# A fourth column chunk of gate and up by seven products, and one written-out order for all units

## The chip, the cores and the metric

The kernel runs on one core of one Trainium2 chip. The metric is device microseconds of one execution, as the median of several. The engines are named as in the profile: PE is the matrix engine (TensorE; PEld is its loading of the stationary operand), DVE is VectorE, ACT is ScalarE, POOL is GpSimd, and SP is SyncE, which here only issues transfers.

## The reference, cut to what matters

One decoder layer on 256 tokens of width 1024: attention and a convolution side by side, an output projection, and a gated feed-forward part. The change touches the last line alone.

```python
D_MODEL = 1024
SEQ = 256
D_FF = -(-8 * D_MODEL // (3 * 256)) * 256        # 2816

    x = x + jnp.concatenate([attn, conv], axis=-1) @ w_out[l]
    h = rms_norm(x, norm2_g[l])
    x = x + (jax.nn.silu(h @ w_gate[l]) * (h @ w_up[l])) @ w_down[l]
```

## The kernel before

**Arithmetic.** Everything is float32 in and out. PE multiplies in a reduced float32 form, so each operand is split into a rounded high part and the rest, and one product of a 128-row block is three matmuls: high by high, high by low, low by high (`product`, L729 to L735). The activations stand still in PE, the weights move through in 512 columns. The activations are 256 tokens, so two token blocks (i = 0, 1); the width of 1024 is two halves (kh = 0, 1) of four blocks of 128.

**Weights.** They come from HBM as blocks of 128x2048 (1 MB), issued by SP into a ring of four buffers (`raw`) or, for three of the four blocks of a shared chunk, into one of three home buffers (`big_h`, `big_l`, `side`). Each block has two pieces of 128x1024. `feed` (L271) prepares pieces ahead of PE: ACT copies the piece to its rounded high part (`wh`, L278), DVE subtracts that from the piece to get the rest (`wl`, L283). Both go into rings of seven buffers (`WGT`), and `feed(at + LEAD)` asks ahead of a unit for the piece four places on. When the second piece of a block is through, the next load is issued.

**Units.** The feed-forward part is a row of units, each 12 matmuls of 128x512. The 2816 columns of gate and up are cut into chunks of 512, 512, 512, 256, 512 and 512 (`WIDTHS`, numbered 0 to 5):

- A plain chunk of 512 is 8 units `("g", c, z, kh, a)`: gate or up (z), half of the width (kh), one piece each. They add into banks `fg`. Chunk 3, of 256 columns, has gate and up in one block: 4 units `("h", 3, 0, kh, a)`.
- A shared chunk takes gate and up of both token blocks by seven products instead of eight (Winograd's form of Strassen's): units `("s", c, j)`, j = 0 to 6, two pieces each. The banks are U (products 0, 2, 4, 6), V (1, 5) and W (3). The four weight blocks are b11, b21 (gate) and b12, b22 (up). Product 0 uses b11, product 3 b21, product 5 b22. Products 1 and 2 use b11 + b12 and that sum plus b22, made by DVE in place (L277). Product 4 uses b12 + b22, and product 6 the sum of all four with b21: these two are made by accumulating transfers that POOL issues (L291), two pieces each. Between products ACT copies U and V out (`s`, L867), and DVE combines them (`c`, L872, L878, L885).
- The down projection is 22 rows `("f", f)` of 128 columns of the activations, one piece each, adding into four banks `pd`. The last four rows wait until the end and are then done bank by bank.

Once gate and up of a chunk are there, ACT takes the silu (`sf`, `sg`, L807), DVE multiplies (`ac`, L822), PE turns the result by transposes (`aT`, L813), ACT copies it (`act`, L816) and DVE makes its low part (`act`, L818); the rows f of that chunk need them.

**Order.** Python's order of these calls is the order on every engine: nothing is moved afterwards. `_order` (L71) writes the units; `_plan` derives from it the list of pieces, which loads follow which piece, and which home a block takes. A home passes from a chunk to the next: after product 4 its buffer takes the next chunk's b11, after product 5 the next b12, after product 6 the next b22. `_order` writes all of chunk 0 plain, then three stages, each with a shared chunk woven into others by a string of turns:

```python
    stage(1, chunk(2), "spspspspspspspp")
    stage(4, half + rows(0, 8), MIXED)
    stage(5, rows(8, 16), "spspspspspspspp")
    return order + rows(16, NF)
```

The banks of U and V, of `aT` and W, and of `fg` and `pd` come from pools of two, two and four; a bank can be written anew only when its last reader is through. Small delays such as `EVICT` count steps of two products and set where a copy or a combination stands between the pieces.

Of the kernel before, what the change touches and what calls it, by code (L numbers as in the profile page):

```python
# [25 lines left out]
NF = FF // P  # L26
# [35 lines left out]
SUMS_WAIT = 6  # L62
WIDTHS = (W, W, W, T, W, W)
STARTS = (0, 512, 1024, 1536, 1792, 2304)
SHARED = (1, 4, 5)
HOMES = ("big_h", "big_l", "side")
FIRST_TURN = 3
MIXED = "psppspssppsppspsppp"


def _order():  # L71

    chunk = lambda c: [("g", c, z, kh, a) for z in range(2) for kh in range(2) for a in range(2)]
    rows = lambda a, b: [("f", f) for f in range(a, b)]
    order = [("g", 0, z, kh, a) for kh in range(2) for z in range(2) for a in range(2)]

    def stage(c, others, turns):
        others = iter(others)
        j = iter(range(7))
        for turn in turns:  # L80
            order.append(("s", c, next(j)) if turn == "s" else next(others))

    half = [("h", 3, 0, kh, a) for kh in range(2) for a in range(2)]
    stage(1, chunk(2), "spspspspspspspp")
    stage(4, half + rows(0, 8), MIXED)
    stage(5, rows(8, 16), "spspspspspspspp")
    return order + rows(16, NF)


def _plan():  # L90
# [9 lines left out]
    for i in range(14):  # L100
        sources += [(i, 0, None, ()), (i, 1, None, (("load",),))]
    quarters = [[block[c, z, kh] for z in range(2) for kh in range(2)] for c in SHARED]
    for n, (b11, b21, b12, b22) in enumerate(quarters):
        for j, b in enumerate((b11, b12, b22)):
            homes[b] = HOMES[(n + j) % 3]
    for kind, *unit in _order():
        if kind != "s":
            i, a = (base + unit[0] // 2, unit[0] % 2) if kind == "f" else (block[tuple(unit[:3])], unit[3])
            if a == 0:
                loads.append(i)  # L110
            sources.append((i, a, None, (("load",),) if a else ()))
            continue
        c, j = unit
        n = SHARED.index(c)
        b11, b21, b12, b22 = quarters[n]
        after = (None,) * 4 if n + 1 == len(SHARED) else quarters[n + 1]
        i, add, more, then = ((b11, None, None, None), (b11, b12, (b12, b22), None), (b11, b22, (b11, b21), None),
                              (b21, None, None, "load"), (b12, None, None, after[0]), (b22, None, None, after[2]),
                              (b11, None, None, after[3]))[j]
        if i == b21:  # L120
            loads.append(i)
        for a in range(2):
            acts = (("add",) + more,) if more else ()
            if a and then is not None:
                acts += (("load",),) if then == "load" else (("home", then),)
            sources.append((i, a, add, acts))
# [72 lines left out]
def _build(nc, tc, t, ctx):  # L199
# [742 lines left out]
    for kind, *unit in _order():  # L942
        feed(at + LEAD)
        if kind in "gh":
            plain_unit(*unit)
        elif kind == "s":
            shared_unit(*unit)
            at += 1
        elif unit[0] < NF - LAST:
            for i in range(NT):  # L950
                for n in range(2):
                    row(unit[0], i, n, wpart(at, n))
        else:
            last[unit[0]] = at
        at += 1
# [66 lines left out]
```

## Time and profile before

| | |
|---|---|
| median of 3 runs | 287.84 us (287.68 to 288.38) |
| the profiled execution | 287.53 us |
| its span, first to last instruction | 285.7 us |
| granted clock of PE | 1.000 |
| busy: PE, DVE, ACT, POOL | 280.8, 226.0, 181.6, 26.9 us |
| moved by the transfers | 63.01 MB, mean 221 GB/s |

The busy times are sums over the span; an engine that is busy for less than the span may still be the one that others wait for in some stretch. Matmuls overlap in the records (each is shown longer than its share), so the chain of work in order of time is the better clock for PE. The numbers of the feed-forward part start at 104.40 us, where its first unit begins.

### The profile page before, as it was taken

The numbers are of one execution on the slowest core, as the hardware profiler recorded it, in microseconds if no ns is written. First come the engines' busy times: TensorE is split into PE (matmuls) and PEld (weight loads), VectorE is DVE, ScalarE is ACT, GpSimd is POOL, SyncE is SP. The second block draws the span as 40 slices with busy tenths as digits, with TensorE's granted clock in tenths as the row PEclk, the third lists the DMA queues.
The fourth block names the chain that finished last, engine by engine and source line by source line (L and its number), as shares of the span: only waits on it lengthen the run. The fifth ranks groups of instructions, "written<-read, shape, count | busy, mean of one in ns | idle before, by whom it ended". The sixth has DMA issues, their size and how long they took to land.

```text
span 285.7 us, 3692 instructions
## 1 busy us (share of the span) xinstructions
PE 280.8 (98%) x1314; PEld 228.1 (80%) x1314; DVE 226.0 (79%) x339; ACT 181.6 (64%) x271; POOL 26.9 (9%) x50
## 2 busy tenths in 40 slices
PE   8999999999999999999999999999999999999994
PEld 6878877778788888888888888888888888888883
DVE  3899994998994957999997769997787896887211
ACT  5777668978837778655987454796455496656000
POOL 0004464001000000010200011200001020000000
PEclk9999999999999999999999999999999999999999
DMA  7999967743633588459999656699864699400012
GB/s 235 418 412 334 408 217 259 281 150 87 271 148 147 219 299 365 147 167 214 198 381 388 272 158 116 181 237 403 311 255 135 131 241 338 142 6 2 0 59 87
DMA packets 12308, 63.01 MB, mean 221 GB/s; under 512 B 1761, under 2 KB 2369, under 8 KB 6530
## 3 DMA queue, kind: packets, MB, share of 16 engines
q1 hardware_dynamic: 9874, 54.93, 51.1%
q0 software_dynamic: 2272, 7.85, 14.6%
q8 instruction: 10, 0.16, 0.2%
q14 instruction: 8, 0.07, 0.1%
q10 hardware_dynamic: 144, 0.00, 0.0%
HBM read 61.53 MB, written 1.05 MB: 219 GB/s over the span
## 4 chain that ended last, share of the span: by engine, by line
PE 98%; DVE 0%; issue 0%
PE pd L732 21%; PE p L694 20%; PE fg L732 19%; PE U L732 11%; PE po L732 8%; PE V L732 6%; PE W L732 3%; PE aT L813 2%; PE warm L347 1%; PE S L533 1%; PE pT L563 1%; PE O L714 1%; PE x2T L755 1%; PE cv L301 0%; PE cv L303 0%; PE cv L302 0%
## 5 line engine op out<-in xcount | busy, mean ns | idle before, releaser
L278 ACT ACTIVATE wh<-raw 128x1024 fp32r<-128x1024 f32 x108 | 111.4, 1057 | 41.6 <-DVE raw L277 19.8
L283 DVE TENSOR_TENSOR wl<-raw,wh 128x1024 fp32r<-128x1024 f32 x108 | 129.2, 1220 | 10.0 <-ACT wh L278 9.4
L732 PE MATMUL pd<-wh,act 128*128 128x512 f32 x176 | 57.2, 393 | 0.0
L732 PE MATMUL fg<-wh,g 128*128 128x512 f32 x160 | 52.2, 393 | 0.0
L732 PEld LDWEIGHTS pd<-wh,act 128*128 128x128 f32 x176 | 33.0, 188 | 6.8
L732 PEld LDWEIGHTS fg<-wh,g 128*128 128x128 f32 x160 | 30.0, 188 | 6.1
L732 PE MATMUL pd<-wl,act 128*128 128x512 f32 x88 | 34.3, 389 | 0.0
L694 PE MATMUL p<-wh,xh 128*128 128x512 f32 x80 | 33.0, 412 | 0.0
L694 PE MATMUL p<-wh,xl 128*128 128x512 f32 x80 | 31.3, 392 | 0.0
L732 PE MATMUL fg<-wl,g 128*128 128x512 f32 x80 | 31.1, 389 | 0.0
L694 PE MATMUL p<-wl,xh 128*128 128x512 f32 x80 | 26.6, 393 | 0.0
L291 POOL DMA_DIRECT2D raw<-w x12 | 10.6, 880 | 155.9 <-DVE raw L277 131.5
L732 PEld LDWEIGHTS pd<-wl,act 128*128 128x128 f32 x88 | 16.6, 188 | 3.3
L694 PEld LDWEIGHTS p<-wh,xh 128*128 128x128 f32 x80 | 15.1, 189 | 3.5 <-issue 0.7
L818 DVE TENSOR_TENSOR act<-aT,act 128x512 fp32r<-128x512 f32 (+1 forms) x12 | 7.7, 644 | 12.9 <-ACT act L816 12.9
L694 PEld LDWEIGHTS p<-wl,xh 128*128 128x128 f32 x80 | 15.1, 189 | 3.3 <-DVE wl L283 0.4
L694 PEld LDWEIGHTS p<-wh,xl 128*128 128x128 f32 x80 | 15.0, 188 | 3.1
L732 PEld LDWEIGHTS fg<-wl,g 128*128 128x128 f32 x80 | 15.0, 188 | 2.9
L816 ACT ACTIVATE act<-aT 128x512 fp32r<-128x512 f32 (+1 forms) x12 | 6.6, 558 | 14.8 <-PE aT L813 14.8
L732 PE MATMUL U<-wh,g 128*128 128x512 f32 x48 | 15.8, 390 | 0.0
L277 DVE TENSOR_TENSOR raw<-raw,raw 128x1024 f32<-128x1024 f32 x12 | 14.6, 1218 | 0.0
L732 PE MATMUL po<-wh,mixh 128*128 128x512 f32 x32 | 12.6, 395 | 0.0
(184 smaller groups left out, 409.9 us busy)
## 6 DMA issues: line engine op xcount, KB each, us to landing
raw<-w SPq DMA_DIRECT2D x45, 1024.0 KB, 5.8
raw<-w POOLq DMA_DIRECT2D x12, 512.0 KB, 5.6
first<-first SPq DMA_DIRECT2D x8, 384.0 KB, 5.6
xtok<-xtok SPq DMA_DIRECT2D x2, 512.0 KB, 9.1
x<-xtok SPq DMA_DIRECT2D x2, 512.0 KB, 7.2
out<-o SPq DMA_DIRECT2D x4, 256.0 KB, 2.0
inv<-inv POOLq DMA_DIRECT2D x1, 768.0 KB, 9.1
c_glub<-glub SPq DMA_DIRECT2D x1, 512.0 KB, 10.8
```

The source lines that it names most:

```text
L277: nc.vector.tensor_tensor(src, src, blocks[add][:, cut(a)], op=ALU.add)
L278: nc.scalar.activation(dst[0], src, AF.Copy)
L283: nc.vector.tensor_tensor(dst[1], src, dst[0].bitcast(F32), op=ALU.subtract)
L291: nc.gpsimd.dma_start(blocks[to][:, cut(a)], t["w"][more - 2][:, cut(a)], accum_op=ALU.add)
L347: nc.tensor.matmul(warm[:, 0:T], zeros[:, 0:P], zeros, start=True, stop=True)
L533: nc.tensor.matmul(banks[a][:, out], G["qT"][rows, j, q], G["kT"][rows, j, k], start=True, stop=True)
L563: nc.tensor.transpose(b[:, a * P:(a + 1) * P], p[:, a * P:(a + 1) * P], ident)
L694: nc.tensor.matmul(banks[i], (xh, xh, xl)[a][:, kt, sls[i]], w[a % 2], start=kt == 0 and a == 0, stop=kt == KT - 1 and a == 2 - (order[-1] ...
L732: nc.tensor.matmul(bank, l, r, start=start and a == 0, stop=stop and a == 2, skip_group_check=on)
L813: nc.tensor.transpose(b[:, a, :], u[:, a * P:(a + 1) * P], ident)
L816: nc.scalar.activation(hi, b[:, 0:nf, :], AF.Copy)
L818: nc.vector.tensor_tensor(lo, b[:, 0:nf, :], hi.bitcast(F32), op=ALU.subtract)
```

## The change

Chunk 2 (columns 1024 to 1536) is no longer plain: it becomes a shared chunk like 1, 4 and 5, by seven products. All units of the feed-forward part after it are written in one string, `TURNS`, in which p is the next plain unit or row and s the next product of the shared chunks in their order. The plain units are chunk 0, the half chunk 3, and the rows; rows 12 and 13 (of chunk 3) are drawn forward to stand after row 3.

```diff
-SHARED = (1, 4, 5)
+SHARED = (1, 2, 4, 5)
 HOMES = ("big_h", "big_l", "side")
 FIRST_TURN = 3
-MIXED = "psppspssppsppspsppp"
+TURNS = "pppppppppspsppssspssppspssspsspsppspssspsspspspssspspssppppppp"
 
 
 def _order():
 
-    chunk = lambda c: [("g", c, z, kh, a) for z in range(2) for kh in range(2) for a in range(2)]
-    rows = lambda a, b: [("f", f) for f in range(a, b)]
-    order = [("g", 0, z, kh, a) for kh in range(2) for z in range(2) for a in range(2)]
-
-    def stage(c, others, turns):
-        others = iter(others)
-        j = iter(range(7))
-        for turn in turns:
-            order.append(("s", c, next(j)) if turn == "s" else next(others))
-
-    half = [("h", 3, 0, kh, a) for kh in range(2) for a in range(2)]
-    stage(1, chunk(2), "spspspspspspspp")
-    stage(4, half + rows(0, 8), MIXED)
-    stage(5, rows(8, 16), "spspspspspspspp")
-    return order + rows(16, NF)
+    plain = [("g", 0, z, kh, a) for kh in range(2) for z in range(2) for a in range(2)]
+    plain += [("h", 3, 0, kh, a) for kh in range(2) for a in range(2)]
+    plain += [("f", f) for f in (*range(4), 12, 13, *range(4, 12), *range(14, NF))]
+    units = {"p": iter(plain), "s": iter([("s", c, j) for c in SHARED for j in range(7)])}
+    return [next(units[turn]) for turn in TURNS]
```

The line numbers of everything behind `_order` fall by ten (L283 becomes L273, L818 becomes L808).

On VectorE before, this stands in chunk 4 from the sum for product 1's second piece to the second piece of product 2 (raw is a weight block, wl a piece's low part, ac a gated product, act a turned low part; numbers tell buffers apart):

```order
L277 TENSOR_TENSOR raw_1539<-raw_1539,raw_1580 128x1024
L283 TENSOR_TENSOR wl_1736<-raw_1539,wh_1735 128x1024
L822 SCALAR_TENSOR_TENSOR ac_1777<-fg_1611,rstd_1263,sf_1604 128x512
L283 TENSOR_TENSOR wl_1764<-raw_1539,wh_1763 128x1024
L277 TENSOR_TENSOR raw_1539<-raw_1539,raw_1630 128x1024
L283 TENSOR_TENSOR wl_1780<-raw_1509,wh_1779 128x1024
L818 TENSOR_TENSOR act<-aT_1790,act 128x4x128
L818 TENSOR_TENSOR act<-aT_1810,act 128x4x128
L277 TENSOR_TENSOR raw_1539<-raw_1539,raw_1630 128x1024
L283 TENSOR_TENSOR wl_1797<-raw_1539,wh_1796 128x1024
L283 TENSOR_TENSOR wl_1826<-raw_1539,wh_1825 128x1024
```

On VectorE now, the same place in the new chunk 2, from the sum for product 1's first piece on (raw_1543 is its b11, raw_1586 its b12, raw_1619 its b22):

```order
L267 TENSOR_TENSOR raw_1543<-raw_1543,raw_1586 128x1024
L273 TENSOR_TENSOR wl_1675<-raw_1374,wh_1674 128x1024
L267 TENSOR_TENSOR raw_1543<-raw_1543,raw_1586 128x1024
L273 TENSOR_TENSOR wl_1689<-raw_1543,wh_1688 128x1024
L808 TENSOR_TENSOR act<-aT_1707,act 128x4x128
L812 SCALAR_TENSOR_TENSOR ac_1728<-c_1640,rstd_1263,sg_1713 128x512
L267 TENSOR_TENSOR raw_1543<-raw_1543,raw_1619 128x1024
L273 TENSOR_TENSOR wl_1716<-raw_1543,wh_1715 128x1024
L267 TENSOR_TENSOR raw_1543<-raw_1543,raw_1619 128x1024
L273 TENSOR_TENSOR wl_1737<-raw_1543,wh_1736 128x1024
L808 TENSOR_TENSOR act<-aT_1750,act 128x4x128
L273 TENSOR_TENSOR wl_1757<-raw_1543,wh_1756 128x1024
```

The piece of a row or plain unit that stood between the two products (wl_1780) is gone from this place, since products 1, 2 and 3 now follow each other; the evictions of the chunk before stand here as they did.

On ScalarE before, from V's first copy (s_1490) to the silu rows of chunk 2's gate (sf), in the first shared chunk (s_1533 is the copy of U between products 2 and 4):

```order
L867 ACTIVATE s_1490<-V_1394 128x512
L278 ACTIVATE wh_1492<-raw_1136 128x1024
L278 ACTIVATE wh_1505<-raw_1184 128x1024
L278 ACTIVATE wh_1517<-raw_1184 128x1024
L867 ACTIVATE s_1533<-U_1393 128x512
L278 ACTIVATE wh_1535<-raw_1285 128x1024
L278 ACTIVATE wh_1548<-raw_1301 128x1024
L278 ACTIVATE wh_1558<-raw_1301 128x1024
```

On ScalarE now, the same place (s_1580 is the copy of U between products 2 and 4; raw_1301 holds product 5's pieces, sf are the silu rows of the half chunk):

```order
L857 ACTIVATE s_1509<-V_1416 128x512
L268 ACTIVATE wh_1511<-raw_1184 128x1024
L268 ACTIVATE wh_1529<-raw_1184 128x1024
L268 ACTIVATE wh_1539<-raw_1285 128x1024
L797 ACTIVATE sf_1551<-fg_1394,rstd_1263 128x256
L797 ACTIVATE sf_1553<-fg_1395,rstd_1263 128x256
L268 ACTIVATE wh_1555<-raw_1301 128x1024
L268 ACTIVATE wh_1568<-raw_1301 128x1024
L857 ACTIVATE s_1580<-U_1415 128x512
```

The copy of U now stands behind both pieces of product 5 and the half chunk's silu rows; before, it stood right behind the pieces of product 4.

## The prediction

> **What bounds the kernel now.** I read the page first, then the waits of the matrix engine, the chain that ended last, the windows of the feed-forward part, and the vector engine's timeline there.
>
> ```profile
> span 285.7 us, 3692 instructions
> PE 280.8 (98%) x1314; PEld 228.1 (80%) x1314; DVE 226.0 (79%) x339; ACT 181.6 (64%) x271; POOL 26.9 (9%) x50
> PE warm L347 <- DVE one L330: 1.0, 1, 1.0
> ```
>
> TensorE (PE) is busy 280.8 of 285.7 us. The third row is all that the list of its waits holds: 1.0 us, at the very start. The chain in order of time shows the feed-forward part (start, length, what; the order of its units is in the code):
>
> ```profile
> 104.40 4.08 PE fg L732 x18
> 108.49 0.87 PE x2T L755 x8
> 109.36 17.70 PE fg L732 x78
> 127.06 2.72 PE U L732 x12
> 129.78 2.72 PE fg L732 x12
> 136.58 0.44 PE aT L813 x4
> 193.86 0.22 PE aT L813 x2
> 194.08 1.39 PE pd L732 x6
> 201.16 5.44 PE pd L732 x24
> 266.98 15.02 PE pd L732 x66
> ```
>
> One unit, plain (fg), shared (U) or row (pd), is 12 matmuls and 2.72 us; the pieces follow each other without a hole. So the part is a row of 63 units, and its end is set by their count as long as PE never waits. The rival for the bound is VectorE:
>
> ```profile
> 120.00:150.00 30.00, 30.00 (x138) 24.84 (x137) 29.95 (x31) 21.79 (x27) 3.57 (x4) 1.00 0.87 250
> 150.00:255.00 105.00, 105.00 (x477) 86.81 (x477) 85.79 (x86) 66.06 (x76) 6.98 (x8) 1.00 0.72 225
> ```
>
> Columns: length, then busy time of PE, PE's loads, DVE, ACT, POOL, then PE's granted clock, DMA share, GB/s. In the first shared chunk DVE is busy 29.95 of 30 us and PE still 30.00; later DVE has 18% free. The granted clock is 1.00, so no term below is about the clock.
>
> **The change part by part.** *Removed.* Columns 1024 to 1536 took 8 plain units and now take 7 products: 63 units become 62, 12 matmuls fewer. The transposes stay 44. That is -2.72 us of PE, all of it on the path.
>
> *Added on the engines beside PE.* Prices (DVE rows: start, length, what):
>
> ```profile
> L283 DVE TENSOR_TENSOR wl<-raw,wh 128x1024 fp32r<-128x1024 f32 x108 | 129.2, 1220 | 10.0 <-ACT wh L278 9.4
> 119.79 1.22 DVE L283 TENSOR_TENSOR wl<-raw,wh 128x1024 fp32r<-128x1024 f32 x1
> 123.87 1.22 DVE L277 TENSOR_TENSOR raw<-raw,raw 128x1024 f32<-128x1024 f32 x1
> 125.00 1.22 DVE L283 TENSOR_TENSOR wl<-raw,wh 128x1024 fp32r<-128x1024 f32 x1
> 131.43 1.22 DVE L283 TENSOR_TENSOR wl<-raw,wh 128x1024 fp32r<-128x1024 f32 x1
> 132.56 0.75 DVE L822 SCALAR_TENSOR_TENSOR ac<-fg,rstd,sf 128x512 f32<-128x512 f32 x1
> 133.22 1.22 DVE L277 TENSOR_TENSOR raw<-raw,raw 128x1024 f32<-128x1024 f32 x1
> 139.56 0.68 DVE L818 TENSOR_TENSOR act<-aT,act 128x512 fp32r<-128x512 f32 x1
> 140.16 1.21 DVE L283 TENSOR_TENSOR wl<-raw,wh 128x1024 fp32r<-128x1024 f32 x1
> 194.53 0.42 DVE L818 TENSOR_TENSOR act<-aT,act 128x256 fp32r<-128x256 f32 x1 [1.58 <-ACT act L816]
> 194.87 0.68 DVE L872 TENSOR_TENSOR c<-W,s 128x512 f32<-128x512 f32 x1
> 195.47 1.22 DVE L283 TENSOR_TENSOR wl<-raw,wh 128x1024 fp32r<-128x1024 f32 x1
> 140.27 2.97 ACT L278 ACTIVATE wh<-raw 128x1024 fp32r<-128x1024 f32 x3
> 143.11 0.61 ACT L867 ACTIVATE s<-U 128x512 f32<-128x512 f32 x1
> 143.59 3.20 ACT L278 ACTIVATE wh<-raw 128x1024 fp32r<-128x1024 f32 x3
> 120.44 2.00 ACT L278 ACTIVATE wh<-raw 128x1024 fp32r<-128x1024 f32 x2
> 126.44 1.25 ACT L807 ACTIVATE sf<-fg,rstd 128x512 f32<-128x512 f32 x2
> ```
>
> What counts is the step from start to start: 1.13 us for a subtract or a sum of 1024 columns (123.87 to 125.00), 0.66 for L822, 0.60 for L818 and for the c rows, 0.34 for the half L818; on ACT 0.95 for a wh (2.97 = 2 x 0.95 + 1.06) and 0.48 for a copy. A shared chunk has 14 pieces where a plain one has 8, plus 4 sums, 3 c rows and 3 copies. So DVE gets 10 x 1.13 + 3 x 0.60 = 13.1 us more, ACT 6 x 0.95 + 3 x 0.48 = 7.1. POOL issues 4 more accumulating transfers; SP issues as many loads as before, in another order. In 120 to 255 DVE goes from 29.95 + 85.79 = 115.7 of 135 us to 128.8 of 132.3: 97%. PE then hides DVE only if the written-out order spreads the work, so I added the rows up in their new order.
>
> *The running sum.* Up to DVE's row at 119.79 both programs run the same. After it I add steps in the order of the changed program, insert a wait where a row needs a product or a transpose of PE, and set each subtract's end against the matmul that reads it, at 2.72 us a unit. For the program of before, the same sum puts the pieces where the timeline has them, to about half a microsecond. Its thinnest place there: the subtract at 131.43 ends at 132.65 and PE reads it in the unit at 135.22, after that unit's first matmul (2.72/12 = 0.23): 2.8 us, and PE did not wait.
>
> In the changed program the thinnest place is the new chunk's third product. DVE's last wait ahead of it is for the half transpose in unit 16. Units counted from 0, unit 9 starts at 129.78, units 9 to 16 and two transposes of 0.44 bring unit 16's middle to 151.06; its transpose ends at 151.28, and the DVE row follows 0.45 later (193.86 + 0.22 to 194.53) at 151.7 and is through at 152.1. Then come ten subtracts and four sums (14 x 1.13), five rows of 0.60, one of 0.34, two of 0.66: 20.5 us, and with a subtract's last 0.09 the end is at 172.7. PE reads that piece in the second half of unit 25: unit 17 starts at 152.86 (unit 16 end 152.64 and 0.22), eight units and two transposes of 0.44 give 175.5, half a unit and one matmul more 177.1. Cover: 4.4 us. The last chunk (2304 to 2816) has the same shape: from its wait for V in unit 41 (end 222.6) eleven subtracts and sums, three rows of 0.60 and two of 0.66 end at 238.3, read at 242.75: 4.4 again. Elsewhere the sum leaves 4.5 to 12. So DVE's 13.1 us cost nothing; what hides them is idle time of before, and if the cover is gone each microsecond late costs PE one.
>
> *Products that PE must wait to overwrite.* U is copied by ACT between the third and the fifth product. In the first shared chunk only one unit now stands between them (two before). The copy comes behind a wh whose buffer PE frees at the end of unit 14 (146.98 by the same count): 147.02 + 0.95 + 0.59 gives 148.6, and the fifth product starts at 149.70: 1.1 us, the smallest cover of all. The half chunk's units now follow the first chunk's at once (unit 8, 127.06) and need its gate banks; ACT's two silu rows there now stand ahead of the first wh that waits for a sum: three wh from 120.44 and 1.25 for the pair (the row at 126.44) end at 124.6, 2.4 us before. Cost of both: nothing, or at most about a microsecond each.
>
> *Transfers.*
>
> ```profile
> raw<-w SPq DMA_DIRECT2D x45, 1024.0 KB, 5.8
> raw<-w POOLq DMA_DIRECT2D x12, 512.0 KB, 5.6
> DMA to landing us min/median/max: 4.7/5.8/12.9
> 132.00:134.00 2.00, 2.00 (x11) 1.65 (x10) 2.00 (x3) 0.69 (x1) 0.00 (x0) 1.00 1.12 195
> 196.00:198.00 2.00, 2.00 (x10) 1.67 (x9) 1.94 (x3) 2.00 (x4) 0.00 (x0) 1.00 1.04 438
> ```
>
> Plain loads fill the queues at 438 GB/s, accumulating ones at 195: four more of 512 KB are 4 x 2.7 = 10.8 us of DMA time. 0.87 x 30 + 0.72 x 105 = 101.7 of 135 becomes 112.5 of 132.3, 85%. The home buffers now pass from chunk to chunk in 5 to 7 units. The tightest is the last chunk's first block: its buffer comes free at 211.1 by the running sum, ACT wants it at 219.3, and DVE's cover there adds 4.4. It may take 12.6 us; the median load takes 5.8, the longest of 45 took 12.9. Cost nothing.
>
> What an issue on POOL costs a VectorE that is busy with two-input rows:
>
> ```profile
> 181.72 8.18 DVE L283 TENSOR_TENSOR wl<-raw,wh 128x1024 fp32r<-128x1024 f32 x7
> 183.47 0.87 POOL L291 DMA_DIRECT2D raw<-w  x1 [8.06 <-ACT wh L278]
> ```
>
> Seven subtracts would take 6 x 1.13 + 1.22 = 8.00; with this issue and the next one inside they took 8.18, so an issue costs DVE 0.09 us, and four of them 0.4 of the 4.4. [...]
>
> **The sum.** -2.72 and nothing back: span 285.7 - 2.7 = 283.0. The profiled execution took 287.53 with 1.8 outside the span, 0.3 under the median of 287.84; carried to the median the forecast is **285.1 us**. The tail stays: three rows instead of four stand between the last shared unit and the four deferred rows, and the last transposed block is ready about 267.8, read from 273.3.
>
> **Rivals.**
>
> *A bank comes free late.* Against it: covers of 1.1 and 2.4 us. For it: the first is thinner than any buffer's. If ACT runs 2 us behind there, PE loses 1: 286.2. Chance 0.08.
>
> *The gain is used up by late home blocks.* For it: the DMA share goes up, and three hand-overs are shorter. [...] It needs the first block of each of the three later chunks to land after about 13.5 us, a little beyond the longest of 45, for 0.9 us each: 2.7 back, 287.8. Chance 0.09.
>
> *VectorE becomes the bound: slower.* Place: the third products of the three later shared chunks. DVE's subtract waits for ACT's copy, which is fed only one piece ahead; 9.4 us of such waits stand in the quoted L283 row. If each of the 22 rows of the thin stretch waited 0.25 us, it would be 5.5 us late; over 4.4 each microsecond is PE's, at three places. It decides against the kernel from 3.6 us of PE waits (2.72 + 0.3%), 5.6 us late at each; at 6 us late the time is 287.84 - 2.72 + 3 x 1.6 = 289.9. Against it: in 120 to 150, the densest stretch before, DVE waited 0.05 us. Chance 0.07.
>
> **How the numbers follow.** About 0.3% is what a measurement of this kernel can tell from no change, 0.86 us here. The forecast holds with 0.76 and the bank rival is also faster by more than 0.3%: 0.84 faster, 0.09 same, 0.07 slower. The range runs from 284.5 (the gain and the lowest run's scatter) to 286.8 (1.7 us of waits at the banks): it takes in 0.84.
>
> **What would show it.** Right: PE's units 2.72 us each with no new waits, span 283.0, DVE near 10 in every window from 120 to 250. Wrong: PEld or PE waits on wl L273 near 177, 210 or 243, on an ACT copy near 149.7, or DVE waiting for a raw load near 219. A unit count other than 62, or a lower granted clock, would break the first term itself.

## The result, and the profile after

| | runs | median us | profiled execution: us, span, last `o` to the end of the span |
|---|---|---|---|
| before | 4 | 287.81 (287.68 to 288.38) | 287.53, 285.7, 3.68 |
| after | 4 | 285.82 (285.07 to 286.28) | 285.87, 284.1, 4.85 |

The ratio after to before is 0.9932, 95% interval 0.9916 to 0.9948: faster by 2.0 us, where 2.7 had been forecast. Spans are given to 0.1 us here, so the last column is good to 0.05. Two places of the trace tell nearly all of it. The first is the end of PE's work, seen at the last `o` (VectorE's add of the last bank; start, length, what), before and after:

```profile
282.02 0.69 DVE L961 TENSOR_TENSOR o<-pd,x 128x512 f32<-128x512 f32 x1 [2.03 <-PE pd L732]
```

```profile
span 284.1 us, 3708 instructions
PE 277.7 (98%) x1302; PEld 225.6 (79%) x1302; DVE 238.3 (84%) x352; ACT 189.2 (67%) x280; POOL 30.4 (11%) x54
PE warm L337 <- DVE one L320: 1.0, 1, 1.0
129.69 2.72 PE U L722 x12
279.25 0.69 DVE L951 TENSOR_TENSOR o<-pd,x 128x512 f32<-128x512 f32 x1 [2.03 <-PE pd L722]
```

The last unit ends 2.77 us earlier, for one unit of 2.72 less. The waits of PE still hold nothing in the feed-forward part (the third row, and one more of 0.3 us that is not shown, are in the first 5 us). The second place is the wait of SP's queue for the last output (time, count, longest) and the time from issue to landing of the four outputs, before and after:

```profile
SPq L1017 <- DMA out<-o: 1.2, 1, 1.2
DMA to landing us min/median/max: 2.0/2.0/2.0
```

```profile
SPq L1007 <- DMA out<-o: 2.4, 1, 2.4
DMA to landing us min/median/max: 2.0/2.0/3.2
```

This wait is 1.2 us longer: the last output took 3.2 us from issue to landing instead of 2.0. So in this execution, of 2.77 us, about 1.2 were lost after the last unit.

The engines beside PE (the windows; length, busy PE, PE's loads, DVE, ACT, POOL, clock, DMA share, GB/s), and the two places that the prediction called thinnest, with the units that read them. The cover is the time from a subtract's end to the matmul that reads it:

```profile
120.00:252.00 132.00, 132.00 (x600) 109.24 (x599) 126.12 (x127) 93.92 (x110) 14.05 (x16) 1.00 0.85 251
```

```profile
171.78 9.16 DVE L273 TENSOR_TENSOR wl<-raw,wh 128x1024 fp32r<-128x1024 f32 x8
175.65 2.72 PE U L722 x12
237.97 8.03 DVE L273 TENSOR_TENSOR wl<-raw,wh 128x1024 fp32r<-128x1024 f32 x7
242.87 2.72 PE W L722 x12
```

VectorE is busy 126.1 of 132 us, and the DMA share is 0.85. The first subtract of the row at 171.78 ends at 173.0, and PE reads it at 175.65 + 1.36 + 0.23 = 177.2: cover 4.2 us. The first at 237.97 ends at 239.2, read at 242.87 + 0.23 = 243.1: 3.9.

### The profile page after: what moved, and what is told of

Read it like the earlier page. It is cut to its first block, busy times and chain, and to the rows that moved or that the text cites. A ratio compares the mean times of both kernels' runs of the same rounds, so it can differ in the third digit from the quotient of the medians.

```text
span 284.1 us, 3708 instructions
## 1 busy us (share of the span) xinstructions
PE 277.7 (98%) x1302; PEld 225.6 (79%) x1302; DVE 238.3 (84%) x352; ACT 189.2 (67%) x280; POOL 30.4 (11%) x54
## 4 chain that ended last, share of the span: by engine, by line
PE 96%; DMA 1%; ACT 0%; DVE 0%; issue 0%
PE pd L722 21%; PE p L684 20%; PE U L722 15%; PE fg L722 12%; PE po L722 8%; PE V L722 8%; PE W L722 4%; PE aT L803 2%; PE S L523 1%; PE pT L553 1%; DMA first<-first 1%; PE O L704 1%; PE x2T L745 1%; PE cv L291 0%; PE cv L293 0%; PE cv L292 0%
## 5 line engine op out<-in xcount | busy, mean ns | idle before, releaser
L268 ACT ACTIVATE wh<-raw 128x1024 fp32r<-128x1024 f32 x114 | 117.9, 1057 | 36.1 <-DVE raw L267 19.9
L273 DVE TENSOR_TENSOR wl<-raw,wh 128x1024 fp32r<-128x1024 f32 x114 | 136.0, 1219 | 5.5 <-ACT wh L268 4.6
L281 POOL DMA_DIRECT2D raw<-w x16 | 14.0, 878 | 158.8 <-PE fg L722 61.8
L722 PE MATMUL fg<-wh,g 128*128 128x512 f32 x96 | 30.4, 392 | 0.0
L722 PE MATMUL U<-wh,g 128*128 128x512 f32 x64 | 21.6, 393 | 0.0
L722 PEld LDWEIGHTS fg<-wh,g 128*128 128x128 f32 x96 | 18.0, 188 | 3.7
L267 DVE TENSOR_TENSOR raw<-raw,raw 128x1024 f32<-128x1024 f32 x16 | 19.5, 1219 | 0.1
L722 PE MATMUL fg<-wl,g 128*128 128x512 f32 x48 | 18.7, 390 | 0.0
L722 PEld LDWEIGHTS U<-wh,g 128*128 128x128 f32 x64 | 12.0, 188 | 2.4
L722 PE MATMUL po<-wh,mixl 128*128 128x512 f32 x32 | 12.5, 391 | 0.0
```

Of the source, the lines that this page charges most:

```text
L267: nc.vector.tensor_tensor(src, src, blocks[add][:, cut(a)], op=ALU.add)
L268: nc.scalar.activation(dst[0], src, AF.Copy)
L273: nc.vector.tensor_tensor(dst[1], src, dst[0].bitcast(F32), op=ALU.subtract)
L281: nc.gpsimd.dma_start(blocks[to][:, cut(a)], t["w"][more - 2][:, cut(a)], accum_op=ALU.add)
L722: nc.tensor.matmul(bank, l, r, start=start and a == 0, stop=stop and a == 2, skip_group_check=on)
```

## The experiments

What was open was the missing 0.7 us. The theory: the row of units gave all it should, and the tail took some back. The rivals: waits of PE in executions that were not profiled, or a cover that is in truth used up.

**The changed kernel again.** No edit.

> The changed kernel once more, to size the 0.7 us by which 285.82 missed 285.1. Theory (row of units): the feed-forward part gives back the whole 2.72 us (last o starts 279.25 in the first profile of it, 2.77 earlier), and what is missing lies behind the last unit, where the last output took 3.2 us to land instead of 2.0; if that is scatter, this run's last o starts at 279.2 to 279.3 again, while the time from there to the end of the span is anywhere from 3.6 to 4.9, and the median comes out between 285.0 and 285.9. Rival A (the tail is systematic: the changed kernel's last output always lands about 1.2 us later): landing 3.2 again, median 285.8 or more. Rival B (PE waits in the feed-forward part in the other runs): last o later than 279.5 in this profile, with waits of PE there.

Median 286.28, ratio 0.9948 (0.9934 to 0.9962).

```profile
279.65 0.69 DVE L951 TENSOR_TENSOR o<-pd,x 128x512 f32<-128x512 f32 x1 [2.03 <-PE pd L722]
SPq L1007 <- DMA out<-o: 2.4, 1, 2.4
```

The last `o` is 0.4 us later in this execution because the whole feed-forward part starts 0.4 later; PE waits nowhere in it. The span ends at 284.5, again some 4.85 us after the last `o`: the long tail is systematic (rival A). In the ratios of the three measurements of this tail (0.9932, 0.9948 and, further down, 0.9957) it is worth 0.6 to 1.4 us against the kernels with a short tail below (0.9907 and 0.9911); the first four executions, one of them at 285.07, show the least of it.

**The order alone**: three shared chunks, chunk 2 plain, all written out.

```diff
-SHARED = (1, 2, 4, 5)
+SHARED = (1, 4, 5)
-TURNS = "pppppppppspsppssspssppspssspsspsppspssspsspspspssspspssppppppp"
+TURNS = "ppppppppsqsqsqsqsqsqsqqppppppppppppspssspsspspspssspspssppppppp"
     # (cut: one line that gives q, chunk 2's eight plain units)
```

> The written-out order without the fourth shared chunk: 63 units again (21 shared, 42 plain), columns 1024 to 1536 plain and ahead of the rows. Theory: the end is set by the count of units, so the last o starts at 281.9 to 282.1 and the median is 287.8 +- 0.4, ratio to before 1.000 +- 0.002, though VectorE gets 13 us less than in the changed kernel. Rival C (the order itself brings something): below 287.2. Rival A says the same span from last o to end as in the changed kernel (4.8), since the end of the order is the same: 288.9.

Median 287.69, ratio 1.0001 (0.9991 to 1.0012): an order written out brings nothing by itself, and 63 units cost what 63 units cost. Its last `o` starts at 281.91 and the span ends at 285.6: a short tail, 3.69, with the same end of the order. So it isn't the end of the order that makes the tail long.

**More VectorE work at the thinnest place**: three subtracts more.

```diff
-            nc.vector.tensor_tensor(dst[1], src, dst[0].bitcast(F32), op=ALU.subtract)
+            for _ in range(4 if j == 63 else 1): nc.vector.tensor_tensor(dst[1], src, dst[0].bitcast(F32), op=ALU.subtract)
```

> The changed kernel with the subtract of the second piece of the new chunk's third product done 4 times over (same result): 3 x 1.13 = 3.4 us more VectorE work just at the place that the prediction called the thinnest, 4.4 us of cover (4.2 by the trace). Theory: 0.8 us of cover is left, PE does not wait, time equal to the changed kernel's within 0.3 us, last o at 279.2 to 279.4. Rival D (the running sum is too kind by over 1 us there, or the cover is used up in some runs): 1 to 3.4 us slower than the changed kernel, with PE waiting for wl near 177.

Median 285.09, ratio 0.9907 (0.9893 to 0.9921): the cover holds, and with *more* work the kernel is 1.2 us *faster* than without.

```profile
279.34 0.69 DVE L951 TENSOR_TENSOR o<-pd,x 128x512 f32<-128x512 f32 x1 [2.03 <-PE pd L722]
SPq L1007 <- DMA out<-o: 1.2, 1, 1.2
```

PE ends where it did, and the tail is the short one. The packets around the last output tell more. The profile after lists two queues of the kind `instruction` (packets, MB, share); the trace gives this name and the sizes, and that the packets are code is my reading of it:

```profile
q8 instruction: 10, 0.16, 0.2%
q14 instruction: 9, 0.07, 0.1%
```

In both traces of the changed kernel an 8192-byte packet on q14 begins 0.99 and 1.00 us after the output's first packet. In the first of them that is at 281.79, where the output's last data packet ends. One of the output's sixteen 4-byte packets stands behind it: it begins at 1.30 us, where the last one of the kernels with a short tail begins at 0.81 to 0.83. In this run with three subtracts more, q14's last packet comes 5.6 us *ahead* of the output.

**Which engine's instructions move the packet?** Three tiny memsets more on VectorE at the start of the program, 15 on VectorE in the kernel before, three tiny activations more on ScalarE:

```diff
-    nc.vector.memset(one, 1.0)
+    for _ in range(4): nc.vector.memset(one, 1.0)        # f1, on the changed kernel
+    for _ in range(16): nc.vector.memset(one, 1.0)       # f2, on the kernel before
-    nc.scalar.activation(table, one, AF.Sigmoid)
+    for _ in range(4): nc.scalar.activation(table, one, AF.Sigmoid)   # f3, on the changed kernel
```

> The changed kernel with three more tiny memsets on VectorE at the very start (the one memset done 4 times over), no work added at the thin place. In the changed kernel's two profiles an 8 KB transfer of the instruction kind lies among the last output's packets and that output lands 3.2 us after its issue; with 3 more subtracts on VectorE that transfer came 6.6 us earlier, the output landed in 2.0 and the time was 285.09. Theory (VectorE's own code is fetched in pieces of 8 KB, and by its count of instructions one of these fetches falls on the last output): landing 2.0, from last o to the end of the span 3.6 to 3.7, median 285.1 +- 0.2. Rival A2 (the length of VectorE's code has nothing to do with it; the delay of the subtracts moved something else): landing 3.2, median 286.2.

> The kernel before with 15 more tiny memsets on VectorE at the very start, so that its VectorE program is as long as the changed kernel's (13 more rows in the profile, and 2 more that only wait). Theory: the fetch now falls on the last output here too: landing 3.2, from last o to the end 4.8 to 4.9, median 288.9 +- 0.3, ratio to before 1.004. Rival A2: landing 2.0, 287.7, ratio 1.000.

> The changed kernel with three more tiny activations on ScalarE at the start. Theory (the fetch is VectorE's): the fetch stays on the last output, landing 3.2, 286.2 +- 0.3. Rival A3 (the fetch belongs to ScalarE, or any change of the start moves it): landing 2.0, 285.1.

| kernel | VectorE rows in the profile | q14's last packet, from the last output's first | SP's wait for it | last `o` to end | median us | ratio to before |
|---|---|---|---|---|---|---|
| before | 339 | -56.4 | 1.2 | 3.68 | 287.32 in these rounds | |
| before, 15 memsets more | 354 | +1.01 | 1.7 | 4.14 | 288.46 | 1.0042 (1.0030 to 1.0054) |
| order alone | 339 | -52.6 | 1.2 | 3.69 | 287.69 | 1.0001 (0.9991 to 1.0012) |
| after | 352 | +0.99 | 2.4 | 4.85 | 285.82 | 0.9932 (0.9916 to 0.9948) |
| after, 3 activations more | 352 | +1.00 | 2.4 | 4.86 | 286.12 | 0.9957 (0.9944 to 0.9970) |
| after, 3 memsets more | 355 | -5.9 | 1.2 | 3.71 | 284.76 | 0.9911 (0.9898 to 0.9924) |
| after, 3 subtracts more | 355 | -5.6 | 1.2 | 3.66 | 285.09 | 0.9907 (0.9893 to 0.9921) |

The fine windows show the same, after ahead of after with three memsets (of the 16 KB that begin in this 0.3 us of the first, half is the packet on q14, at 281.79):

```profile
281.50:281.80 0.30, 0.00 (x0) 0.00 (x0) 0.00 (x0) 0.00 (x0) 0.00 (x0) 1.00 0.16 55
```

```profile
279.19 0.69 DVE L951 TENSOR_TENSOR o<-pd,x 128x512 f32<-128x512 f32 x1 [2.03 <-PE pd L722]
SPq L1007 <- DMA out<-o: 1.2, 1, 1.2
281.50:281.80 0.30, 0.00 (x0) 0.00 (x0) 0.00 (x0) 0.00 (x0) 0.00 (x0) 1.00 0.01 0
```

Three instructions more on VectorE, at the start as at the thin place, move the packet away and the time down by 1.2 to 1.4 us; three on ScalarE do neither; 15 on VectorE put it onto the output of the kernel before and cost 1.14 us there. In that kernel's profiled execution, the fastest of its five (288.01), the packet begins just behind the last 4-byte packet and the tail grew by 0.46 only, less than the forecast 1.2. So in these runs the number of VectorE's instructions sets when this packet comes, and on the last output it goes with a time longer by about a microsecond. That it is a fetch of VectorE's code was the theory; the trace does not show what the packet holds. Why the landing is 1.2 us later with a packet of 0.31 us is shown in part. In the trace the landing of an output is sixteen updates of a semaphore. In the changed kernel fifteen come by 281.98, each about 0.35 us behind its 4-byte packet as in the kernels with a short tail; only the last is late, at 283.14. Of its delay, 0.48 is the late 4-byte packet, and 0.69 is that the update comes 1.04 us behind that packet. What holds the update back is not seen.

**Where the cover ends**: 4, 5 and 7 subtracts more at the thin place (the diff as above, with 5, 6 and 8).

> The second piece of the new chunk's third product subtracted 5 times over: 4 x 1.26 - 4.2 = 0.8 us late. With 6 subtracts PE waited 2.1 and in most executions the clock then stood at 0.50 for some 3 us, so that the median was 3.9 above the kernel with the short tail. Theory (a short wait leaves the clock alone): PE waits 0.8, clock 1.00, 284.8 + 0.8 = 285.6. Rival (any wait halves the clock in part of the executions): median above 286.5 or executions of two kinds.

> The changed kernel with the second piece of the new chunk's third product subtracted 6 times over. In the run with 8 a repeat took 1.26 us, PE waited 4.6 us (8.8 less a cover of 4.2), and then its granted clock stood at 0.50 for 6.5 us, which cost 3.3 us more. Here: 5 x 1.26 - 4.2 = 2.1 us late. Theory (a wait is worth its own length unless PE is idle for long enough that its clock is halved, about 4 us): PE waits 2.1, clock 1.00 throughout, 2.1 above the kernel without the fetch on its tail: 287.2 (VectorE's program is 5 longer, so the tail is the short one). Rival (any wait of some us halves the clock): 2.1 + 1.5 to 3.3, so 288.7 to 290.5.

> The same with 8 subtracts in place of one: 7 x 1.13 = 7.9 us more. Theory: 7.9 - 4.2 = 3.7 to 3.8 us late, PE waits 3.8 us in one piece for that wl near 177 and nowhere else, last o at 283.0, time 3.8 us above the changed kernel's. Rival D: more than 4.8. Rival E (VectorE's work is not what PE would ever wait for; the ring of copies is fed far enough ahead): under 2.

PE's waits in the feed-forward part, with 4, 5 and 7 more, all of them:

```profile
PE U L722 <- DVE wl L273: 0.9, 1, 0.9
```

```profile
PE U L722 <- DVE wl L273: 2.1, 1, 2.1
```

```profile
PE U L722 <- DVE wl L273: 4.6, 1, 4.6
```

With 7 more, the row of subtracts at the thin place is:

```profile
172.22 17.98 DVE L273 TENSOR_TENSOR wl<-raw,wh 128x1024 fp32r<-128x1024 f32 x15
```

Less the 9.13 us of eight subtracts (7 x 1.13 + 1.22), a repeat took 1.26 us (it rewrites the same buffer; why it takes 0.13 more than another subtract is not shown), so 4 x 1.26 - 4.2 = 0.8, 5 x 1.26 - 4.2 = 2.1 and 7 x 1.26 - 4.2 = 4.6: the cover is 4.2 us to within 0.1 (the third expectation had 1.13 for a repeat). But the times are 286.17 (ratio 0.9947, 0.9934 to 0.9960), 288.65 (1.0037, 1.0022 to 1.0051) and 292.06 (1.0137, 1.0118 to 1.0156). By ratio the first is about 1.1 above the kernels with the short tail, its own wait; the second is 3.6 to 3.7 above (3.9 above the three memsets in the same rounds), the third 6.5 to 6.6 (7.0 above the three subtracts in the same rounds). The windows say why. With 5 more, and with 7 more (clock is the last but two):

```profile
177.00:178.00 1.00, 0.45 (x2) 0.03 (x1) 0.98 (x1) 1.00 (x3) 0.00 (x0) 1.00 0.00 0
178.00:179.00 1.00, 0.00 (x0) 0.00 (x0) 0.97 (x2) 0.44 (x1) 0.00 (x0) 1.00 0.00 0
180.00:181.00 1.00, 1.00 (x5) 0.81 (x4) 1.00 (x2) 0.00 (x0) 0.87 (x1) 0.69 0.06 16
181.00:182.00 1.00, 1.00 (x3) 0.80 (x3) 1.00 (x2) 0.49 (x1) 0.00 (x0) 0.50 0.60 33
183.00:184.00 1.00, 1.00 (x4) 0.79 (x3) 1.00 (x2) 0.06 (x2) 0.00 (x0) 0.61 1.01 197
184.00:185.00 1.00, 1.00 (x6) 0.81 (x5) 1.00 (x2) 1.00 (x1) 0.00 (x0) 1.00 1.10 229
```

```profile
181.00:182.00 1.00, 0.00 (x0) 0.00 (x0) 0.98 (x1) 0.00 (x0) 0.00 (x0) 0.59 0.00 0
187.00:188.00 1.00, 1.00 (x3) 0.73 (x3) 1.00 (x2) 0.60 (x1) 0.00 (x0) 0.50 0.89 213
188.00:189.00 1.00, 1.00 (x6) 0.79 (x5) 1.00 (x2) 0.46 (x1) 0.00 (x0) 1.00 0.88 360
```

After the wait of 2.1 us the granted clock stands at 0.50 from about 180.4 to 183.8, 3.4 us, which by the clock costs 1.7 us: 2.1 + 1.7 = 3.8. After 4.6 it stands there from 181.2, still in the wait, to 188.0, 6.8 us. That execution was the slowest of four (292.76, mean clock 0.987); the other three have a mean clock of 0.992 to 0.994, so about half as long a stretch. After 0.9 it stayed at 1.00. The "about 4 us" of the second expectation was my estimate from the one wait of 4.6; no run shows it, and 2.1 was enough here. In the run with 5 more, 3 of 12 executions took 287.0 to 287.5 at a mean clock of 0.999 or 1.000, and the others 288.6 to 289.1 at 0.991 or 0.992: the former fit the wait alone (284.8 + 2.1), the latter the wait and one stretch at half clock.

**The fourth chunk without the spread order**: the products of the last three shared chunks back to back (with the three memsets).

```diff
-TURNS = "pppppppppspsppssspssppspssspsspsppspssspsspspspssspspssppppppp"
+TURNS = "pppppppppspsppssspssppsssssssssssssssssssssppppppppppppppppppp"
```

> The fourth shared chunk without the spread order: from unit 22 on, the 21 products of the last three shared chunks back to back, then all rows (with the three memsets at the start). The count of units stays 62. Theory (the written-out order is what hides VectorE's 13 us): VectorE now has more steps in that stretch than the products last; the same running sum as in the prediction gives 6.1 us of PE waits there, each for a wl, none over 2.2 us, so 284.8 + 6 = 290.9, and up to 3 more for each stretch in which the clock halves: 290 to 295. Rival (the count of units alone decides, the order is of no account): 284.8.

Median 307.07, ratio 1.0684 (1.0662 to 1.0706): 22 us slower than in the spread order, for the same 62 units. All of PE's waits in the part:

```profile
PE U L722 <- DVE c L875: 8.6, 2, 5.4
PE V L722 <- ACT sg L797: 3.1, 2, 1.6
PE U L722 <- ACT s L857: 1.9, 3, 1.2
PE U L722 <- DVE c L868: 0.8, 1, 0.8
```

```profile
178.83 8.65 DMA raw<-w
210.09 6.02 DMA raw<-w
```

The theory had the direction, and the wrong place. PE never waited for `wl`: each chunk needs U and V of the chunk before, and the steps that empty them stand in VectorE's and ScalarE's queues behind sums and subtracts of home blocks that are still on the way (the two rows of the chain). 14.4 us of waits, a mean clock of 0.94 from 165 to 245. So two of the prediction's rivals, banks that come late and home blocks that come late, are real in this kernel, and it is the order that keeps them away.

**Evictions one step later.**

```diff
-EVICT = 1
+EVICT = 2
```

(with the three memsets). The copies of U then take in a part of the product after, so of this kernel only the time is read.

> Copies and evictions one step later than in the changed kernel (EVICT 2 in place of 1, with the three memsets at the start). It tests the smallest cover of the prediction: U's copy in the first shared chunk ended 1.2 us ahead of the fifth product in the trace (148.5, 149.69). One wh more ahead of it (0.95 us and what that wh waits for its buffer) makes it about 0.3 us late. Theory: PE waits 0.2 to 0.6 us for s L857 in the first shared chunk, little or nothing elsewhere: 284.8 to 285.6. Rival (the cover is larger than worked out): no wait, 284.8. Rival (banks come late in every shared chunk): four waits, 286 or more.

Median 291.76, ratio 1.0140 (1.0116 to 1.0164). The theory was far too small.

```profile
PE aT L803 <- DVE ac L812: 1.9, 1, 1.9
PE fg L722 <- ACT sf L797: 1.6, 1, 1.6
PE U L722 <- ACT s L857: 0.7, 1, 0.7
```

```profile
126.90 1.06 ACT wh L268
127.96 0.58 ACT sf L797
128.59 3.05 PE fg L722 x12
```

The expected wait for `s` is there with 0.7. But at unit 8 the silu rows now stand behind the first `wh` that waits for a sum, and the cover of 2.4 us, which the prediction put down to their standing ahead of it, turns into a wait of 1.6. By ratio the kernel is 6.6 us above those with the short tail. The waits add up to 4.4, with one of 0.2 for `wh`. Behind the wait of 1.9, which ends at 242.8, the clock stood at 0.50 from 243.9 to 247.3: 1.7 us more in this execution (mean clock 0.994). Two of the five executions had a mean clock of 1.000 and took 290.8 and 291.0. Half a microsecond to one stays open.

**The last output in two halves** on two queues (with the three memsets).

```diff
-            nc.vector.tensor_tensor(o, pd[i, n], x2[:, i, n * W:n * W + W], op=ALU.add)
-            nc.sync.dma_start(t["out"][i][:, n * W:n * W + W], o)
+            for h, q in ((slice(0, T), nc.sync), (slice(T, W), nc.scalar)) if i and n else ((slice(0, W), nc.sync),):
+                nc.vector.tensor_tensor(o[:, h], pd[i, n][:, h], x2[:, i, n * W:n * W + W][:, h], op=ALU.add)
+                q.dma_start(t["out"][i][:, n * W:n * W + W][:, h], o[:, h])
```

> The changed kernel with the three memsets, and the last output added and sent in two halves of 256 columns, the first by SP's queue, the second by ScalarE's. A test of what the tail consists of, and a try for a faster kernel. Theory (the tail is one add of 0.69, an issue, and a landing of 2.0 of which the transfer is 0.8): the first half starts 0.3 us earlier, the second lands with half the data: 0.2 to 0.4 us less, 284.4 to 284.6. Rival (the landing is all fixed cost): the second half's add ends 0.1 later, 284.8 to 284.9.

Median 284.52, ratio 0.9896 (0.9878 to 0.9913). Its interval overlaps that of the three memsets alone (0.9898 to 0.9924), so the further 0.2 us are not settled. The two halves (KB, median us to landing):

```profile
out<-o SPq DMA_DIRECT2D x1, 128.0 KB, 1.8
out<-o ACTq DMA_DIRECT2D x1, 128.0 KB, 1.8
```

Half the data landed in 1.8 us instead of 2.0, so most of a landing does not depend on the size here. Either is a kernel that beats both; what they share is the three memsets.

## Why the prediction was right, and where it was off

*One unit less, all on the path.* Right: -2.77 us at the last `o` (2.72 for the unit, the rest from a part that starts at 104.32 instead of 104.40), and the order alone, with 63 units, is at 1.0001.

*VectorE's 13 us are hidden.* Right. Worked out were 128.8 us busy and covers of 4.4; the trace has 126.1, and 4.2 and 3.9. The added subtracts found the edge at 4.2. The price beyond it was not what I thought: "each microsecond late costs PE one" holds for 0.9 us, while 2.1 cost 3.6 to 3.9 in the median and 4.6 cost 6.5 to 7.0, because the granted clock fell to 0.50 at the wait. Whether the slower rival, three waits of 1.6 us, would have been dearer than its 289.9 is not shown: in the run with later evictions a wait of 1.6 us left the clock at 1.00, one of 1.9 did not.

*The banks.* Right: U's copy in the first shared chunk ended 1.1 us ahead of the fifth product (148.55 and 149.69), as forecast; the gate banks were free 2.5 ahead of unit 8 (124.46 and 126.97; forecast 2.4). The copy and the silu rows:

```profile
147.97 0.58 ACT L857 ACTIVATE s<-U 128x512 f32<-128x512 f32 x1
123.21 1.25 ACT L797 ACTIVATE sf<-fg,rstd 128x512 f32<-128x512 f32 x2
```

The later evictions show how little that is. (The bank rival's 286.2 was added up a little high: ACT 2 us behind, less the cover of 1.1, is 0.9 on 285.1, so 286.0.)

*The transfers.* The DMA share of 0.85 came out as worked out. Loads took 7.0 us in the median instead of 5.8, and accumulating ones 6.9 instead of 5.6:

```profile
raw<-w SPq DMA_DIRECT2D x45, 1024.0 KB, 7.0
raw<-w POOLq DMA_DIRECT2D x16, 512.0 KB, 6.9
ACT wh L268 <- DMA raw<-w: 0.5, 1, 0.5
```

The last row is the only wait of ScalarE or VectorE for a load in the feed-forward part: 0.5 us, within the covers.

*POOL's issues.* Two issues fall into the eight subtracts at 171.78 (POOL issues at 171.56 and 173.29, 0.88 and 0.87 long). Without them 7 x 1.13 + 1.22 = 9.13, and they took 9.16: about 0.015 us for an issue, where the prediction had 0.09.

*"The tail stays": the step that failed.* From the last `o` to the end of the span I left 3.68 us as before. It measured 4.85. The prediction gave a reason from the order of the tail's instructions, which is unchanged, and put at nothing whatever else moves data there: with 13 rows more on VectorE the last packet of q14 lies on the last output (it begins 0.99 us after the output's first, where in the kernel before it came 56.4 us ahead). With the packet off it (three memsets more) the ratio is 0.9911 (0.9898 to 0.9924); 285.1 of 287.84, as forecast, is 0.9905. The time of 285.82 was within the range all the same, and that is not because the prediction knew of the tail: its range had been left for waits at the banks, of which there were none.

## What to carry to other kernels

Where one engine is never late, the end is a count: count its instructions, and spend the work on showing that every other stream keeps its cover, piece by piece, banks and home buffers included. Beyond a cover the price can jump: here a wait of 0.9 us on the matrix engine cost its own length, and one of 2.1 us nearly twice as much in most executions, because the granted clock fell to 0.50 behind it. When a change misses by about a microsecond, look at the last transfer too, packet by packet: here an 8 KB packet of another queue lay on it, and three idle instructions moved that off.

## What the runs showed of the hardware

- With an 8192-byte packet of q14, a queue of the kind `instruction`, 0.99 us behind its first packet, the last output landed in 3.2 us instead of 2.0. With three memsets more on VectorE that packet came 5.9 us ahead of the output, and SP's wait for the output was 1.2 us, as in the kernel before, instead of 2.4. Within the spans of before and after, the packets of this kind are of 8192 bytes on q14 (8 and 9 of them) and of 16384 on q8 (10); which engine each of them serves does not show.
- The granted clock fell to 0.50 after a wait of 2.1 us, for 3.4 us, and at one of 4.6 for 6.8; after 0.9 it did not fall. With later evictions it did not fall after a wait of 1.6 us (1.00 from 120 to 150) and did after one of 1.9, for 3.4 us. Why 3 of the 12 executions with 5 subtracts more kept a mean clock of 0.999 or 1.000, with the same work on VectorE, is not shown: only of the profiled one, with 0.992, is the clock known over time.
